# The two directions of a recurrent scan, summed by a transfer that adds in HBM

## The chip, the cores and the metric

The kernel runs on one core of a Trainium2 chip. That core has five engines with a queue each: TensorE (PE, matrix products into PSUM), VectorE (DVE), ScalarE (ACT), GpSimd (POOL) and SyncE (SP), which here only issues transfers. Each engine works through its own queue in order, and waits where another engine or a transfer has not signalled yet. The metric is the time of one launch in device microseconds; less is better. Before the change three runs took 1267.52, 1268.32 and 1270.27 us, a median of 1268.32 us.

## The reference, cut to what matters

The program is a two-layer backbone over 1024 latent tokens and 256 context tokens of width 1024. Layer 0 has a convolution branch A and a branch B, a gated linear recurrence that runs over the tokens in both directions. The change touches branch B alone, and the order of work in branch A's convolution.

```python
def lru_coeffs(u2, p):                     # u2: the input and its reversal
    r = sigmoid(u2 @ w_r + b_r); i = sigmoid(u2 @ w_i + b_i)      # 8 heads of 128
    log_a = -LRU_C * r * softplus(-lam)
    return exp(log_a), sqrt(-expm1(2 * log_a)) * (i * u2)

def rglru_branch(xb, p, h0, with_outputs):
    u = depthwise_conv(xb, p["sconv_w"], p["sconv_b"], (2, 1))    # 4 taps
    a, bx = lru_coeffs(stack([u, u[:, ::-1]]), p)
    hT, hs = lru_scan(a, bx, h0, with_outputs)                    # h = a * h + bx
    return hs[:, :, 0] + hs[::-1, :, 1], hT                       # the sum of the two directions

y_a = silu(layernorm(depthwise_conv(va * sigmoid(vg), conv_w, conv_b))) * silu(ga)   # 31 taps
y_b = rglru_branch(xb, p, h_ctx, True) * silu(gb)
out = concatenate([y_a, y_b]) @ w_out
```

The recurrence runs over the 256 context tokens first, and its last state starts the latent tokens. All products are made in float32 precision out of three matmuls of rounded parts (high by high, high by low, low by high).

## The kernel before

Channels lie on the 128 partitions and tokens along them, so the width of 1024 makes eight blocks j = 0 to 7. The stage at issue is a loop over these blocks (line 903), some 42.5 us a round. In round j TensorE makes, in this order: the gate input `vg` of branch A (two halves of 512 tokens), the value `va` (two halves), then, for block j + 1, the recurrence's input `xb` on the context (`xbc`), and then, interleaved, the gate products of block j (`g`, twelve groups of three matmuls, `gate_steps`) and `xb` of block j + 1 on the latent tokens. Each product of 512 columns is 24 matmuls: for each of eight blocks of the width `hi` by `xh`, `hi` by `xl`, `lo` by `xh`. Weights are loaded raw by SP, and `raw_split` makes their two parts: the high one `wh_...` by a cast on ACT, the low one `wl_...` by a subtraction on POOL. So TensorE's third matmul of a product is the first to need POOL's part.

The recurrence of block j is prepared in round j (gates into the buffers `l`) and finished in round j + 1 as `state`: POOL multiplies the input gate by the input (`rec_input`, one call for each direction: `l<-l,uc`), ACT makes `tanh` of the decay gate into a buffer `roots` (`rec_tanh`, `l<-l,chalf`), then `exp` and the square root, POOL multiplies again (`rec_scaled`, `l<-l,l`), and DVE scans (`rec_scan`: a multiply, then a scan over 256 and one over 1024 tokens, for each direction). At last `rec_sum` (line 877) adds the two directions on DVE and SP stores the sum to `yb_raw[j]` in HBM, from where `gated` (line 1219) reads it in the stage after the loop.

Six buffers `l` of 1280 columns are passed around. After its scans, a state's two results `i0` (forward) and `i1` (backward) become the `roots` of the next state:

```python
998                (r0, i0, r1, i1), (e, f) = state[2], state[3]
999                gates, roots = [e, f, r0, r1], [i1, i0]
```

So the `tanh` of direction 0, early in the round after, writes the buffer that held the backward result of the state before.

DVE also makes branch A's 31-tap convolution, block by block, as single steps of a generator; `fill(n)` puts the next n of them into DVE's queue at the place where it is called. The order on every engine in this stage is the order in which the program is written (each instruction is held behind the last of its engine, `on`). In a round the calls that matter come so: `vg` half 0; `rec_input(state, 1)`; the `first_tap` of the 4-tap convolution on ACT; `rec_tanh(state)`; the split of `va`'s weights; `vg` half 1; `va`; `xbc`; the scans and the sum; the gate products, and after the tenth of their twelve groups (`n == 9`, line 1006) the split of the next `vg` weights and `rec_input(now, 0)`; at the end `fill(6)`.

After the loop come the gate products `gb1` to `gb7` of branch B, with the last state's scans (block 7) among them, then the product `wob` with the gated branch B.

## Time and profile before

| | |
|---|---|
| median of the three runs | 1268.32 us |
| the three runs | 1267.52 to 1270.27 us |
| span of the profiled execution | 1263.6 us, 16209 instructions |
| PE busy | 1249.8 us (99%) |
| DVE busy | 1139.3 us (90%) |
| ACT busy | 653.8 us (52%) |
| POOL busy | 295.7 us (23%) |
| granted TensorE clock, mean | 0.998 |

The profile's times count from the span's start, and the span begins with the first instruction and ends with the last; the time of a run lies about 4.7 us above it (1268.32 against 1263.6). The profiled execution has no other time of its own. Matmuls are pipelined: one of 512 columns is shown with some 0.39 us, though the next one starts 0.23 us after it. In the rows an engine's idle time stands in brackets with what ended it. A transfer's time is counted from its issue to its landing. The loop over the blocks fills the span from about 75 to 414 us; the `gb` products end at about 490 us.

### The profile page before, as it was taken

The numbers are of one execution on the slowest core, as the hardware profiler recorded it, in microseconds if no ns is written. First come the engines' busy times: TensorE is split into PE (matmuls) and PEld (weight loads), VectorE is DVE, ScalarE is ACT, GpSimd is POOL, SyncE is SP. The second block draws the span as 40 slices with busy tenths as digits, with TensorE's granted clock in tenths as the row PEclk, the third lists the DMA queues.
The fourth block names the chain that finished last, engine by engine and source line by source line (L and its number), as shares of the span: only waits on it lengthen the run. The fifth ranks groups of instructions, "written<-read, shape, count | busy, mean of one in ns | idle before, by whom it ended". The sixth has DMA issues, their size and how long they took to land.

```text
span 1263.6 us, 16209 instructions
## 1 busy us (share of the span) xinstructions
PE 1249.8 (99%) x5866; PEld 1035.6 (82%) x5866; DVE 1139.3 (90%) x1746; ACT 653.8 (52%) x952; POOL 295.7 (23%) x176
## 2 busy tenths in 40 slices
PE   9999999999999999999999999999999999999997
PEld 7788888888888888888887878888888888888786
DVE  7799999999999999998978969999899987977975
ACT  8464566656666534237535445744343444644642
POOL 0015364436444547543210023000000000000002
PEclk9999999999999999999999999999999999999999
DMA  9970121112121233442436666344323334759723
GB/s 376 388 254 33 52 65 46 63 43 75 42 84 42 84 119 132 159 150 84 147 112 225 202 206 183 103 136 148 125 94 140 117 125 126 268 199 335 285 71 134
DMA packets 78705, 182.29 MB, mean 144 GB/s; under 512 B 7712, under 2 KB 23328, under 8 KB 78624
## 3 DMA queue, kind: packets, MB, share of 16 engines
q1 hardware_dynamic: 67328, 172.33, 39.8%
q10 hardware_dynamic: 11296, 8.92, 2.2%
q8 instruction: 46, 0.75, 0.2%
q14 instruction: 35, 0.29, 0.1%
HBM read 137.18 MB, written 44.04 MB: 143 GB/s over the span
## 4 chain that ended last, share of the span: by engine, by line
PE 70%; DVE 18%; DMA 7%; issue 2%; ACT 2%; POOL 1%; SPq 0%; POOLq 0%; ACTq 0%; DVEq 0%
PE wob L670 7%; DVE conv L670 5%; PE va L670 5%; PE xb L670 4%; PE vg L670 4%; DVE l L670 3%; PE fold L670 3%; PE g L670 3%; PE qb_v L1153 2%; PE ga L670 2%; PE qb_g L1156 2%; PE ga L161 2%; PE qb_v L1156 2%; PE qb_g L1155 2%; PE qb_g L1153 2%
## 5 line engine op out<-in xcount | busy, mean ns | idle before, releaser
L670 DVE SCALAR_TENSOR_TENSOR conv<-u,sm,conv 128x505 f32<-128x505 f32 (+6 forms) x224 | 153.6, 744 | 1.0
L2045 POOL TENSOR_TENSOR o<-x,rr 128x256 f32<-128x256 f32 (+1 forms) x10 | 9.2, 952 | 448.4 <-ACT rr L2045 448.4
L670 ACT ACTIVATE l<-g,sm 128x512 f32<-128x512 f32 (+1 forms) x96 | 58.7, 619 | 57.7 <-PE g L670 57.0
L670 POOL TENSOR_TENSOR l<-l,l 128x1280 f32<-128x1280 f32 x16 | 47.1, 2967 | 25.6 <-ACT l L670 15.1
L670 PE MATMUL gb<-h0h,wl_gb 128*128 128x512 f32 x128 | 49.9, 390 | 0.4 <-POOL wl_gb L670 0.4
L670 PE MATMUL va<-h0h,wl_va 128*128 128x512 f32 x128 | 49.9, 390 | 0.2 <-DVE wl_va L670 0.2
L98 ACT CAST wq_g<-wr_g 128x512 fp32r<-128x512 f32 x48 | 28.2, 621 | 41.9 <-DMA wr_g<-wg 15.6
L670 PE MATMUL gb<-h0l,wh_gb 128*128 128x512 f32 x128 | 49.8, 389 | 0.0
L670 PE MATMUL gb<-h0h,wh_gb 128*128 128x512 f32 x128 | 49.8, 389 | 0.0
L670 PE MATMUL va<-h0l,wh_va 128*128 128x512 f32 x128 | 49.8, 389 | 0.0
L670 PE MATMUL va<-h0h,wh_va 128*128 128x512 f32 x128 | 49.8, 389 | 0.0
L670 PE MATMUL wob<-ybl,wh_wob 128*128 128x512 f32 x128 | 49.8, 389 | 0.0
L670 PE MATMUL wob<-ybh,wl_wob 128*128 128x512 f32 x128 | 49.8, 389 | 0.0
L670 PE MATMUL wob<-ybh,wh_wob 128*128 128x512 f32 x128 | 49.8, 389 | 0.0
L670 DVE TENSOR_TENSOR_SCAN l<-l,l 128x256 f32<-128x256 f32 (+1 forms) x32 | 48.7, 1521 | 1.1
L670 DVE SCALAR_TENSOR_TENSOR conv<-cL,wsum,conv 128x506 f32<-128x506 f32 (+3 forms) x70 | 48.1, 745 | 0.2
L670 POOL TENSOR_TENSOR l<-l,uc 128x1280 f32<-128x1280 f32 x16 | 47.6, 2999 | 0.0
L98 ACT CAST wq_wo<-wr_wo 128x512 fp32r<-128x512 f32 x48 | 28.6, 620 | 35.5 <-DVE wr_wo L1134 12.4
L98 ACT CAST wq_v<-wr_v 128x512 fp32r<-128x512 f32 x48 | 28.1, 620 | 33.7 <-DMA wr_v<-wfold 16.6
L670 PE MATMUL xb<-h0l,wh_xb 128*128 128x512 f32 x112 | 43.8, 391 | 0.0
L670 PE MATMUL xb<-h0h,wh_xb 128*128 128x512 f32 x112 | 43.8, 391 | 0.0
L670 POOL TENSOR_TENSOR wl_xb<-wr_xb,wh_xb 128x1024 fp32r<-128x1024 f32 x7 | 16.8, 2407 | 114.5 <-ACT wh_xb L670 114.5
(680 smaller groups left out, 4362.5 us busy)
## 6 DMA issues: line engine op xcount, KB each, us to landing
modw<-modW SPq DMA_DIRECT2D x16, 512.0 KB, 10.2
mod<-modT SPq DMA_DIRECT2D x32, 256.0 KB, 3.4
wr_v<-wfold SPq DMA_DIRECT2D x16, 512.0 KB, 4.0
wr_g<-wg SPq DMA_DIRECT2D x16, 512.0 KB, 4.3
wr_wo<-wo SPq DMA_DIRECT2D x16, 512.0 KB, 4.1
mod<-modT SPq DMA_DIRECT2D x14, 512.0 KB, 4.5
y_b<-y SPq DMA_DIRECT2D x24, 256.0 KB, 3.5
y_t<-y SPq DMA_DIRECT2D x24, 256.0 KB, 3.1
```

Of the source, the lines that this page charges most:

```text
L98: return (nc.scalar.copy(hi, src), eng.tensor_tensor(out=lo, in0=src, in1=hi.bitcast(F32), op=sub))
L161: mm(ps, hi[:, kc], xh[k][:, cols], start=(k == 0), stop=False)
L670: last[eng] = f(*args, **kw)
L1153: nc.tensor.matmul(ps, hi, xh[k], start=(first and k == 0), stop=False, skip_group_check=not first)
L1155: nc.tensor.matmul(ps, hi, xl[k], start=False, stop=False, skip_group_check=not first)
L1156: mm = nc.tensor.matmul(ps, lo, xh[k], start=False, stop=(k == KH - 1), skip_group_check=not first)
L2045: tail[eng] = f(*args, **kw)
```

## The change

`rec_sum` goes, and with it DVE's addition of the two directions, eight instructions in all. In its place `rec_store(state, d)` stores one direction. For d = 0 SP writes the forward result to `yb_raw[j]`, right behind the forward scan. For d = 1 POOL issues a transfer of the backward result to the same place that adds to what lies there (`accum_op=add`). In the loop this stands behind the next state's `rec_input(now, 0)`, behind the tenth gate group; the last state's stands behind `at_rest` after its second scan. The `fill` at the end of rounds 1 to 6 rises from 6 to 8 steps, and the one after `gb3`'s product falls from 24 to 18, so that the convolution's steps are the same in number and stand earlier.

```diff
+    def plus(dst, src):
+        on("pool", nc.gpsimd.dma_start, dst, src, accum_op=add)
+
...
-        def rec_sum(st):
-            hs, hb = st[2][1], st[2][3]
-            vec(nc.vector.tensor_tensor, out=hs[:, C:], in0=hs[:, C:], in1=hb[:, C:], op=add)
-            nc.sync.dma_start(yb_raw[st[0]], hs[:, C:])
+        def rec_store(st, d):
+            latent = st[2][2 * d + 1][:, C:]
+            if d == 0:
+                nc.sync.dma_start(yb_raw[st[0]], latent)
+            else:
+                plus(yb_raw[st[0]], latent)
...
             if state is not None:
-                for d in range(2):
-                    rec_scan(state, d)
-                rec_sum(state)
+                rec_scan(state, 0)
+                rec_store(state, 0)
+                rec_scan(state, 1)
             at_rest()
...
                 if n == 9:
                     w = raw_split(raw, name)
                     rec_input(now, 0)
+                    if state is not None:
+                        rec_store(state, 1)
             all_of(steps)
-            fill(19 if state is None else 6)
+            fill(19 if state is None else 6 if final else 8)
...
         gb_product(3, gws[3])
-        fill(24)
+        fill(18)
         rec_scan(state, 0)
+        rec_store(state, 0)
...
         rec_scan(state, 1)
-        rec_sum(state)
         at_rest()
+        rec_store(state, 1)
```

How the queues change is read from the two built programs. First POOL at the end of round 1, before (`wl_vg`, `wl_va`, `wl_xb` are the low parts of weights; `l<-l,uc` are the two calls of `rec_input`):

```order
L670 TENSOR_TENSOR wl_vg_1608<-wr_vg_1471,wh_vg_1607 128x1024
L670 TENSOR_TENSOR l_914<-l_914,uc_1159 128x1280
L670 TENSOR_TENSOR l_911<-l_911,uc_1159 128x1280
L670 TENSOR_TENSOR wl_va_1680<-wr_va_1677,wh_va_1679 128x1024
L670 TENSOR_TENSOR wl_xb_1720<-wr_xb_1717,wh_xb_1719 128x1024
```

and now:

```order
L670 TENSOR_TENSOR wl_vg_1607<-wr_vg_1471,wh_vg_1606 128x1024
L670 TENSOR_TENSOR l_914<-l_914,uc_1159 128x1280
L670 DMA yb_raw_85<-l_912 128x1024
L670 TENSOR_TENSOR l_911<-l_911,uc_1159 128x1280
L670 TENSOR_TENSOR wl_va_1682<-wr_va_1679,wh_va_1681 128x1024
L670 TENSOR_TENSOR wl_xb_1722<-wr_xb_1719,wh_xb_1721 128x1024
```

The adding transfer out of `l_912`, block 0's backward result, stands between the two input products, and everything that POOL does for `va`'s weights is behind it.

Next ACT at the turn from round 1 to round 2, with what each instruction waits for, before (`uc<-xb` is `first_tap`, the two `chalf` rows are `rec_tanh`, `wh_va` is the high part of `va`'s weights):

```order
L670 ACTIVATE l_911<-g_1_1_768_1620,sm 128x512 [waits PE_49]
L670 ACTIVATE uc_1498<-xb_1517,sm 128x1024 [waits PE_49]
L670 ACTIVATE l_912<-l_913,chalf 128x1280 [waits DVE_49,Activation_49]
L670 ACTIVATE l_910<-l_909,chalf 128x1280 [waits DMAHW5_49,Activation_49]
L670 CAST wh_va_1679<-wr_va_1677 128x1024 [waits DMAHW4_49]
```

and now:

```order
L670 ACTIVATE l_911<-g_1_1_768_1620,sm 128x512 [waits PE_49]
L670 ACTIVATE uc_1498<-xb_1516,sm 128x1024 [waits PE_49]
L670 ACTIVATE l_912<-l_913,chalf 128x1280 [waits DMASW0_49,Activation_49]
L670 ACTIVATE l_910<-l_909,chalf 128x1280 [waits DMAHW5_49,Activation_49]
L670 CAST wh_va_1681<-wr_va_1679 128x1024 [waits DMAHW4_49]
```

Nothing has moved here, but one wait is another: the first `tanh`, which writes `l_912`, waited for DVE and now waits for `DMASW0`, the completion of POOL's adding transfer. `DMAHW5` is SP's store out of `l_910`.

Last DVE in round 2, from the scans of block 1 on, before (the scans are printed as SCALAR_TENSOR_TENSOR on `l` with 256 and 1024 columns; `conv` and `u` rows are convolution steps):

```order
L670 SCALAR_TENSOR_TENSOR l_911<-l_909,l_911 128x1280
L670 SCALAR_TENSOR_TENSOR l_911<-l_909,l_911 128x256
L670 SCALAR_TENSOR_TENSOR l_911<-l_909,l_911 128x1024
L670 TENSOR_TENSOR l_914<-l_914,l_911 128x1024
L670 SCALAR_TENSOR_TENSOR edge_junk,edges<-u_1735,sm 128x8
L670 TENSOR_TENSOR cL<-u_1735 128x512
L670 SCALAR_TENSOR_TENSOR conv_0_1632<-cL,wsum,u_1400 128x512
L670 SCALAR_TENSOR_TENSOR u_1400<-u_1400,sm,conv_1_1633 128x512
L670 SCALAR_TENSOR_TENSOR conv_1_1633<-cL,wsum,conv_1_1633 128x511
```

and now:

```order
L670 SCALAR_TENSOR_TENSOR l_911<-l_909,l_911 128x1280
L670 SCALAR_TENSOR_TENSOR l_911<-l_909,l_911 128x256
L670 SCALAR_TENSOR_TENSOR l_911<-l_909,l_911 128x1024
L670 SCALAR_TENSOR_TENSOR edge_junk,edges<-u_1737,sm 128x8
L670 TENSOR_TENSOR cL<-u_1737 128x512
L670 SCALAR_TENSOR_TENSOR conv_1_1633<-cL,wsum,conv_1_1633 128x511
```

The addition `l_914<-l_914,l_911` is gone, and the two convolution steps that stood behind `cL` here have moved up, ahead of the scans.

## The prediction

> **What bounds the kernel now.** I read the page's busy shares first, then the busy time by stage, then TensorE's waits.

> ```profile
> PE 1249.8 (99%) x5866; PEld 1035.6 (82%) x5866; DVE 1139.3 (90%) x1746; ACT 653.8 (52%) x952; POOL 295.7 (23%) x176
> ...
> core 0: us, PE busy (x) PEld busy (x) DVE busy (x) ACT busy (x) POOL busy (x), PEclk, DMA share, GB/s
> ...
> 289.10:331.60 42.50, 42.50 (x206) 35.86 (x205) 40.30 (x51) 26.45 (x30) 20.20 (x9) 1.00 0.16 56
> 331.60:374.10 42.50, 42.50 (x206) 35.85 (x205) 42.04 (x55) 26.46 (x30) 20.63 (x9) 1.00 0.20 69
> 374.10:415.00 40.90, 40.90 (x187) 34.02 (x187) 40.38 (x51) 27.84 (x31) 21.48 (x9) 1.00 0.19 60
> 415.00:490.60 75.60, 75.15 (x332) 61.89 (x331) 73.53 (x102) 32.32 (x43) 42.41 (x22) 1.00 0.32 103
> ...
> 600.00:760.00 160.00, 158.69 (x715) 130.56 (x714) 136.72 (x249) 74.92 (x119) 21.50 (x14) 1.00 0.55 179
> ...
> PE gb L670 <- POOL wl_gb L670: 0.4, 1, 0.4
> ```

> The first figure of a window is its length, the second PE's busy time. In the loop's rounds both are equal: TensorE never waits. DVE's 40.30 to 42.04 us a round lie beside it with 0.5 us or more to spare. After the loop PE idles 0.45 us (415 to 490.6, one wait for POOL's `wl_gb`) and 1.31 us (600 to 760). So relief for DVE finds about 1.8 us of TensorE waiting to remove, while any new wait that reaches TensorE is paid in full.

> **What DVE loses and gains.**

> ```profile
> L670 DVE TENSOR_TENSOR l<-l,l 128x1024 f32<-128x1024 f32 x8 | 9.8, 1225 | 0.3
> ...
> L670 DVE SCALAR_TENSOR_TENSOR conv<-u,sm,conv 128x505 f32<-128x505 f32 (+6 forms) x224 | 153.6, 744 | 1.0
> ```

> Eight additions at 1.225 us go, 9.8 us in all. In rounds 1 to 6 two steps more at 0.744 us replace each: 2 x 0.744 - 1.225 = +0.26 us a round, at most 42.04 + 0.26 = 42.3 us of 42.5: still hidden by TensorE. The six steps fewer behind `gb3` give back 4.5 us. I count the relief as 0.7 us of the 1.8 us: the 0.45 us at `wl_gb`, whose chain begins with DVE, and a little of the rest. The bounds are 0 and 1.8 us. Were TensorE's cover gone, the 0.26 us would be paid six times, 1.6 us.

> **The new wait, followed through one turn of the loop.** The backward result's buffer is free for the next round's first `tanh` only when the adding transfer has landed, and that transfer is issued behind the input product. Here are POOL, ACT and PE where round 7 begins:

> ```profile
> 371.56 2.40 POOL L670 TENSOR_TENSOR wl_vg<-wr_vg,wh_vg 128x1024 fp32r<-128x1024 f32 x1 [14.34 <-DVE conv L670]
> ...
> 376.83 3.00 POOL L670 TENSOR_TENSOR l<-l,uc 128x1280 f32<-128x1280 f32 x1
> 379.77 2.43 POOL L670 TENSOR_TENSOR wl_va<-wr_va,wh_va 128x1024 fp32r<-128x1024 f32 x1
> ...
> 375.22 2.61 ACT L670 ACTIVATE l<-l,chalf 128x1280 f32<-128x1280 f32 x2
> 377.74 1.03 ACT L670 CAST wh_va<-wr_va 128x1024 fp32r<-128x1024 f32 x1
> 379.56 0.60 ACT L670 ACTIVATE sg<-vg 128x512 f32<-128x512 f32 x1 [0.78 <-PE vg L670]
> ...
> 384.80 0.39 PE L670 MATMUL va<-h0h,wh_va 128*128 128x512 f32 x1
> 385.02 0.39 PE L670 MATMUL va<-h0l,wh_va 128*128 128x512 f32 x1
> 385.25 0.39 PE L670 MATMUL va<-h0h,wl_va 128*128 128x512 f32 x1
> ```

> The first input product ends at 376.83, where the second begins. Call L the time from there until the transfer has landed and ACT may go on: POOL's own share of the issue, the transfer and its signal. `tanh` began at 375.22; now it begins at 376.83 + L. From its begin to the end of `wh_va` are 377.74 + 1.03 - 375.22 = 3.55 us, then some 0.1 us and 2.43 us of POOL for `wl_va`: 6.08 us. TensorE wants `wl_va` at 385.25, so `tanh` may begin at 379.17 at the latest, and L may be 2.34 us. What is longer is idle time of TensorE:

> stall = L - 2.3 us in each round.

> Queued behind the waiting `tanh` on ACT are the second `tanh`, `wh_va`, the sigmoids `sg` that free `vg`'s PSUM, the cast `uh` that DVE's `ul` needs, and the next weights; behind the transfer on POOL the second input product and `wl_va`. The second input product now ends near 379.83 plus POOL's issue time, so ACT's cast, not POOL, sets `wl_va` as long as L exceeds the issue. The rest has slack: `exp` and the roots move by L + 1.6 us, but TensorE moves by L - 2.3 us too, and ACT had 3.9 us idle ahead of the next context tap.

> ```profile
> 356.33 0.57 ACT L670 ACTIVATE uc<-xbc,sm 128x256 f32<-128x256 f32 x1 [3.90 <-PE xbc L670]
> ...
> 365.29 3.08 DVE L670 TENSOR_TENSOR_SCAN l<-l,l 128x256 f32<-128x256 f32 x2
> ```

> DVE is held at `ul` for about as long as TensorE is, and both move on together. The transfer's other two waits are over by then: the backward scans of the state before end at 368.4, 8 us ahead of 376.83, and the forward store is issued earlier still.

> Seven `tanh` stand behind a transfer: those of rounds 2 to 7 and the last state's among the `gb` products. For the last one the same chain leads to `gb2`'s low weights, with one consequence more:

> ```profile
> 412.94 2.61 ACT L670 ACTIVATE l<-l,chalf 128x1280 f32<-128x1280 f32 x2
> ...
> 413.52 5.91 POOL L670 TENSOR_TENSOR l<-l,uc 128x1280 f32<-128x1280 f32 x2
> ...
> 423.23 5.91 POOL L670 TENSOR_TENSOR l<-l,l 128x1280 f32<-128x1280 f32 x2 [1.45 <-ACT l L670]
> 429.08 2.42 POOL L670 TENSOR_TENSOR wl_gb<-wr_gb,wh_gb 128x1024 fp32r<-128x1024 f32 x1
> ...
> 435.73 0.39 PE L670 MATMUL gb<-h0h,wl_gb 128*128 128x512 f32 x1
> ```

> The first of the two input products ends at 413.52 + 2.96 = 416.48. `tanh` goes from 412.94 to 416.48 + L, so the roots, POOL's scaled products and the `wl_gb` behind them (end 431.50) move by 3.54 + L, to 435.04 + L. TensorE wants them at 435.73 plus its own stall of L - 2.35, 433.38 + L. That is 1.6 us more, once, whatever L is. The last state's own transfer is waited for only by a load of `cH` and by reads of `yb_raw`, which the earlier forward store leaves room for: nothing.

> **How long is L?** The trace has no transfer that adds and none that POOL issues. The nearest rows, with median time to landing at the end:

> ```profile
> yb_raw<-l SPq DMA_DIRECT2D x8, 512.0 KB, 2.6
> wr_vg<-win SPq DMA_DIRECT2D x7, 512.0 KB, 3.5
> modw<-modW SPq DMA_DIRECT2D x16, 512.0 KB, 10.2
> ```

> Below, the plain store of the same tile, 2.6 us: adding cannot be less work. Reading HBM first and writing then would be a load and a store in a row, 3.5 + 2.6 = 6.1 us. Above, the slowest transfers of this size, 10.2 us beside full traffic; here traffic is light (a DMA share of 0.2). I take L = 5.3 us, nearer the sum than the store, since reads and writes of the pieces overlap in part while POOL's issue comes on top. The stall is then 3.0 us.

> [...]

> **The sum.** 7 x 3.0 = 21.0, plus 1.6, minus 0.7: +21.9 us. The profiled span would be 1263.6 + 21.9 = 1285.5 us; the median lies 4.7 us above the span, so 1290 us. With L = 2.6: 7 x 0.3 + 0.9 = 3.0, 1271 us. With L = 10.2: 7 x 7.9 + 0.9 = 56.2, 1324 us.

> **Rivals.** *The transfer is nearly as quick as the store* (L below 3.3). For it: an idle DMA, and the store's 2.6 us. Against it: it reads as well, and POOL must issue it. Stall below 1.0, 1271 to 1279 us.

> *POOL issues the transfer while the product in front still runs.* Then L counts from 373.9, not from 376.83: with L = 5.3 the transfer lands at 379.2, `tanh` may begin until 379.17, and nothing stalls. The 1.6 us at `gb3` go as well, since the roots come 2.96 us earlier. What is left is DVE's relief, 0.7 to 1.8 us: 1266.5 to 1267.6 us. This is the mechanism on the other side, and it decides from an overlap of 2.9 us on. For it: POOL's rows follow each other with no gap, so something of the next instruction is prepared early. Against it: two products in a row take 5.9 us, twice one, so their work does not overlap.

> *TensorE's clock falls in the stalls.* The profile's end shows what idling does:

> ```profile
> 1254.00:1255.00 1.00, 0.61 (x4) 0.52 (x4) 0.59 (x2) 0.30 (x2) 0.31 (x1) 1.00 0.97 322
> ...
> 1257.00:1258.00 1.00, 0.00 (x0) 0.00 (x0) 0.80 (x3) 0.16 (x1) 0.76 (x2) 0.68 0.41 139
> 1258.00:1260.00 2.00, 0.00 (x0) 0.00 (x0) 1.24 (x4) 0.00 (x0) 1.33 (x2) 0.50 0.48 157
> ```

> The granted clock, third from the end, goes from 1.00 to 0.50 some 3 us after dense work stops near 1254.6. If each stall did that, and the clock took as long to return, 3 us at half speed cost 1.5 us more per stall, 10.5 us: 1301 us. Against it: the stall is split, about 0.9 us before the first matmul (`wh_va` at 385.7 instead of 384.80) and the rest before the third. [...]

> **How the numbers follow.** The forecast, with L from 3.3 to 7.0 and a full clock, 1276 to 1303 us, gets 0.66; a longer transfer or a falling clock, 1301 to 1324 us, 0.16; the quick transfer 0.10; the overlapped issue 0.08. Leaving out the overlapped issue, the lower half of the quick case and the far end of the long one, the range is 1274 to 1313 us. About 0.2% or 2.5 us is what a measurement of this kernel can tell from no change, so 1265.8 to 1270.9 us is "same". The overlapped issue falls there or just below it, 0.05 and 0.03, and the quick case ends above. Slower: 0.92.

> **What would show it.** In the changed profile the first `tanh` of rounds 2 to 7 should be released by the transfer of `yb_raw`, some 7 us later in its round than before, and PE should wait for ACT's `wh_va` and POOL's `wl_va`, seven times (`gb` once) about 3 us in all; each round should take 45.5 us instead of 42.5. DVE's 1.225 us additions should be gone with no gain to be seen. If `tanh` begins in time, or PE shows no wait for `va` weights, the central step is wrong; if the transfer's time to landing is far from 5 us, only the size is.

## The result, and the profile after

The changed kernel takes 1300.88 us (median of 4 runs, 1296.27 to 1305.84), the kernel before, on the same chip, 1267.92 us: a ratio of 1.0263, 95% interval 1.0235 to 1.0291. That is 33.0 us more; the forecast was 21.7 us more. The profiled execution took 1300.49 us, with a span of 1298.7 us, 35.1 us above the span of before.

The page of the changed kernel, busy shares and three of its groups (the number behind the last bar is the idle time of the engine just before the group, and what ended it):

```profile
PE 1263.3 (97%) x5866; PEld 1039.9 (80%) x5866; DVE 1136.3 (87%) x1738; ACT 652.8 (50%) x952; POOL 303.8 (23%) x184
...
L670 PE MATMUL va<-h0h,wl_va 128*128 128x512 f32 x128 | 52.7, 412 | 10.4 <-POOL wl_va L670 10.2
...
L670 PE MATMUL va<-h0h,wh_va 128*128 128x512 f32 x128 | 52.4, 410 | 3.6 <-ACT wh_va L670 3.6
...
L670 ACT ACTIVATE l<-l,chalf 128x1280 f32<-128x1280 f32 x16 | 21.0, 1358 | 48.1 <-DMA yb_raw<-l 48.1
```

TensorE, never idle in the loop before, now waits for both parts of `va`'s weights, and ScalarE's `tanh` waits 48.1 us for the transfer of `yb_raw`. DVE's additions are gone and its share is lower, with no gain to be seen. TensorE's waits in total, times and longest:

```profile
PE va L670 <- POOL wl_va L670: 10.2, 6, 1.7
PE gb L670 <- POOL wl_gb L670: 4.5, 3, 1.8
PE va L670 <- ACT wh_va L670: 3.6, 6, 0.8
PE qac_wo L1164 <- DVE wq_wo L99: 2.3, 2, 1.3
```

Round 7 in the order of time, for POOL, ACT and PE, answers to the rows that the prediction shows of before:

```profile
393.98 2.94 POOL L670 TENSOR_TENSOR l<-l,uc 128x1280 f32<-128x1280 f32 x1
396.87 0.84 POOL L670 DMA_DIRECT2D yb_raw<-l  x1
397.48 3.23 POOL L670 TENSOR_TENSOR l<-l,uc 128x1280 f32<-128x1280 f32 x1
405.47 2.36 POOL L670 TENSOR_TENSOR wl_va<-wr_va,wh_va 128x1024 fp32r<-128x1024 f32 x1 [4.76 <-ACT wh_va L670]
...
401.84 2.62 ACT L670 ACTIVATE l<-l,chalf 128x1280 f32<-128x1280 f32 x2 [6.46 <-DMA yb_raw<-l]
404.37 1.03 ACT L670 CAST wh_va<-wr_va 128x1024 fp32r<-128x1024 f32 x1
...
405.45 0.50 PE L670 MATMUL va<-h0h,wh_va 128*128 128x512 f32 x1 [0.44 <-ACT wh_va L670]
405.79 0.40 PE L670 MATMUL va<-h0l,wh_va 128*128 128x512 f32 x1
407.89 0.50 PE L670 MATMUL va<-h0h,wl_va 128*128 128x512 f32 x1 [1.71 <-POOL wl_va L670]
```

The transfer is issued at 396.87, when the first input product has ended, and the `tanh` starts at 401.84: L = 4.97 us here, 5.0 to 5.3 us over the seven turns. `wh_va` and `wl_va` follow in a chain, and TensorE waits 0.44 us for the one and 1.71 us for the other. The round loses more than their sum, 2.7 us: the idle time in brackets counts from the end at which the matmul before is shown, 0.39 us after its start, where the next one would start after 0.23; and behind each wait the second matmul starts 0.34 us after the first (405.45 and 405.79).

But not all turns are alike. Where TensorE's same matmul stands in both traces gives what each stretch lost:

| stretch | lost against before, us |
|---|---|
| up to round 1 | 0.6 |
| rounds 2, 4, 6 | 4.70, 4.53, 4.56 |
| rounds 3, 5, 7 | 2.87, 2.78, 2.72 |
| `gb` products | 7.4 |
| `wob` to the end | 4.9 |
| sum | 35.1 |

The waits are of the same size in every round. What is more in every other one is seen in the windows around the waits of round 2 (first three rows) and of round 3 (last three). A row is a stretch with its length, TensorE's busy time, the matmuls in it and the granted clock; the stretches are 3.41 us long and begin where the clock's records begin and end:

```profile
core 0: us, PE busy (x), PEclk, DMA share, GB/s
170.50:173.91 3.41, 2.67 (x12) 1.00 0.00 0
173.91:177.33 3.42, 1.64 (x6) 1.00 0.00 0
177.33:180.74 3.41, 3.41 (x10) 0.50 0.33 84
...
218.28:221.70 3.42, 2.81 (x12) 1.00 0.00 0
221.70:225.11 3.41, 1.73 (x8) 1.00 0.21 51
225.11:228.52 3.41, 3.41 (x17) 1.00 0.20 51
```

Behind round 2's waits the clock is 0.50 for exactly one stretch (10 matmuls where there are 17 at full clock); behind round 3's it stays at 1.00. It fell so four times, behind the waits of rounds 2, 4 and 6 and of `gb2`. A round with the fall lost 4.60 us on average and one without 2.79, so a fall cost 1.8 us: 3.41 us at half speed are 1.71.

In the `gb` stage there is one more wait, at `gb5`, where the prediction had counted nothing (POOL, then SP's queue, ACT and PE):

```profile
472.86 0.88 POOL L670 DMA_DIRECT2D yb_raw<-l  x1 [8.86 <-DVE l L670]
479.32 3.01 POOL L670 TENSOR_TENSOR ybl<-sb,ybh 128x512 fp32r<-128x512 f32 x2 [5.58 <-DMA yb_raw<-l]
485.88 2.37 POOL L670 TENSOR_TENSOR wl_gb<-wr_gb,wh_gb 128x1024 fp32r<-128x1024 f32 x1 [3.56 <-issue]
...
479.38 0.33 SPq L256 DMA_DIRECT2D cH<-cc  x1
...
483.70 0.63 ACT L257 ACTIVATE cH<-cH 128x512 f32<-128x512 f32 x1 [2.46 <-DMA cH<-cc]
...
484.71 1.04 ACT L670 CAST wh_gb<-wr_gb 128x1024 fp32r<-128x1024 f32 x1
...
485.81 0.50 PE L670 MATMUL gb<-h0h,wh_gb 128*128 128x512 f32 x1 [0.16 <-ACT wh_gb L670]
488.31 0.50 PE L670 MATMUL gb<-h0h,wl_gb 128*128 128x512 f32 x1 [1.77 <-POOL wl_gb L670]
```

POOL's first `ybl` (the low part of block 0's gated branch) waits 5.58 us for the last adding transfer, and SP issues the load of `cH` only when that has landed, too. The second is what reaches TensorE. The load lands some 4 us later, ACT's step on `cH` waits 2.46 us for it, `wh_gb` of `gb5` stands behind that step on ACT, and `wl_gb` behind `wh_gb`; POOL itself stood idle for 3.56 us between `ybl` and `wl_gb`. TensorE waits 0.16 + 1.77 = 1.93 us.

### The profile page after: what moved, and what is told of

It is laid out like the page before. It is cut to its first block, busy times and chain, and to the rows that moved or that the text cites. A ratio compares the mean times of both kernels' runs of the same rounds, so it can differ in the third digit from the quotient of the medians.

```text
span 1298.7 us, 16234 instructions
## 1 busy us (share of the span) xinstructions
PE 1263.3 (97%) x5866; PEld 1039.9 (80%) x5866; DVE 1136.3 (87%) x1738; ACT 652.8 (50%) x952; POOL 303.8 (23%) x184
## 5 line engine op out<-in xcount | busy, mean ns | idle before, releaser
L670 DVE SCALAR_TENSOR_TENSOR conv<-u,sm,conv 128x505 f32<-128x505 f32 (+6 forms) x224 | 152.7, 745 | 0.8
L670 ACT ACTIVATE l<-g,sm 128x512 f32<-128x512 f32 (+1 forms) x96 | 58.5, 618 | 58.0 <-PE g L670 54.5
L670 PE MATMUL va<-h0h,wl_va 128*128 128x512 f32 x128 | 52.7, 412 | 10.4 <-POOL wl_va L670 10.2
L670 POOL TENSOR_TENSOR l<-l,l 128x1280 f32<-128x1280 f32 x16 | 47.6, 2998 | 38.7 <-ACT l L670 38.7
L670 PE MATMUL va<-h0h,wh_va 128*128 128x512 f32 x128 | 52.4, 410 | 3.6 <-ACT wh_va L670 3.6
L670 PE MATMUL gb<-h0h,wl_gb 128*128 128x512 f32 x128 | 50.9, 398 | 4.5 <-POOL wl_gb L670 4.5
L670 PE MATMUL va<-h0l,wh_va 128*128 128x512 f32 x128 | 51.8, 405 | 0.0
L670 DVE TENSOR_TENSOR_SCAN l<-l,l 128x256 f32<-128x256 f32 (+1 forms) x32 | 50.7, 1586 | 1.1
L670 PE MATMUL gb<-h0h,wh_gb 128*128 128x512 f32 x128 | 50.8, 397 | 0.7 <-ACT wh_gb L670 0.7
L670 PE MATMUL gb<-h0l,wh_gb 128*128 128x512 f32 x128 | 50.4, 394 | 0.0
L670 PE MATMUL wob<-ybh,wh_wob 128*128 128x512 f32 x128 | 49.9, 389 | 0.0
L670 PE MATMUL wob<-ybl,wh_wob 128*128 128x512 f32 x128 | 49.9, 389 | 0.0
L670 PE MATMUL wob<-ybh,wl_wob 128*128 128x512 f32 x128 | 49.8, 389 | 0.0
L670 POOL TENSOR_TENSOR l<-l,uc 128x1280 f32<-128x1280 f32 x16 | 49.3, 3085 | 0.0
L670 DVE SCALAR_TENSOR_TENSOR conv<-cL,wsum,conv 128x506 f32<-128x506 f32 (+3 forms) x70 | 47.4, 743 | 0.1
L670 ACT ACTIVATE l<-l,chalf 128x1280 f32<-128x1280 f32 x16 | 21.0, 1358 | 48.1 <-DMA yb_raw<-l 48.1
L670 PE MATMUL xb<-h0l,wh_xb 128*128 128x512 f32 x112 | 43.9, 392 | 0.0
L670 PE MATMUL xb<-h0h,wh_xb 128*128 128x512 f32 x112 | 43.8, 391 | 0.0
L670 PE MATMUL xb<-h0h,wl_xb 128*128 128x512 f32 x112 | 43.6, 389 | 0.0
## 6 DMA issues: line engine op xcount, KB each, us to landing
modw<-modW SPq DMA_DIRECT2D x16, 512.0 KB, 10.2
wr_v<-wfold SPq DMA_DIRECT2D x16, 512.0 KB, 3.8
wr_g<-wg SPq DMA_DIRECT2D x16, 512.0 KB, 4.6
wr_wo<-wo SPq DMA_DIRECT2D x16, 512.0 KB, 4.8
mod<-modT SPq DMA_DIRECT2D x14, 512.0 KB, 4.6
```

Of the source, the lines that this page charges most:

```text
L670: last[eng] = f(*args, **kw)
```

## The experiments

The theory after the result: (1) the next `tanh` waits for the landing of the adding transfer, and only through that do the weights come late; (2) where enough of the wait falls into one of the clock's stretches, TensorE runs the next one at half speed; (3) the last transfer costs the wait at `gb5`. The rivals: the moved convolution steps cost; POOL's issue or the transfer's traffic costs wherever it stands; the clock falls by chance. Every ratio is against runs of the kernel before in the same comparison, medians of 1266.5 to 1267.4 us.

**fills_only**: the convolution steps as changed, the sum back on VectorE.

```diff
                 rec_scan(state, 0)
-                rec_store(state, 0)
                 rec_scan(state, 1)
+                rec_sum(state)
...
                     rec_input(now, 0)
-                    if state is not None:
-                        rec_store(state, 1)
```

and the same for the last state, with `rec_sum` as it was.

> The sum of the two directions goes back to VectorE and SP as before the change; only the other part of the change stays: 8 instead of 6 convolution steps at the end of rounds 1 to 6, and 18 instead of 24 behind the third gb product. Theory (the landing of the adding transfer holds the next tanh, and nothing else costs): 2 x 0.744 = 1.5 us more for VectorE in a round, under TensorE's 42.5 us; the time is that of before, 1266 to 1270 us, with TensorE waiting in no round of the loop. Rival (the moved convolution steps hold VectorE's chain, and through it TensorE): a good part of the 33 us shows here, 1275 us or more.

Measured: 1267.50 us, ratio 0.9994 (0.9983 to 1.0005), and no wait of TensorE in the loop. The steps moved cost nothing and bring nothing.

**transfer_only**: the transfers as changed, the convolution steps as before.

```diff
-            fill(19 if state is None else 6 if final else 8)
+            fill(19 if state is None else 6)
...
-        fill(18)
+        fill(24)
```

> The two transfers stay as changed; the convolution steps go back to 6 in every round and 24 behind the third gb product. Theory (landing): the seven stalls stay as they are, 1298 to 1303 us, within 3 us of the changed kernel. Rival (the moved convolution steps cost): near 1270 us.

Measured: 1302.29 us, ratio 1.0274 (1.0254 to 1.0295). The whole loss is the transfers'. Here L is 5.2 to 5.4 us, and the clock fell behind the waits of rounds 2 (for two stretches), 4, 5, 7 and `gb2`: other rounds than in the changed kernel.

**early**: the same transfer, issued ahead of the split of the `vg` weights.

```diff
                 if n == 9:
+                    if state is not None:
+                        rec_store(state, 1)
                     w = raw_split(raw, name)
                     rec_input(now, 0)
-                    if state is not None:
-                        rec_store(state, 1)
```

> In the loop the adding transfer is issued ahead of the split of the next vg weights and of the first input product instead of behind them; the same transfers, bytes and convolution steps, and the last state's transfer stays where it is. POOL stands idle there, so the transfer starts when the backward scan has ended, some 8 us earlier. Theory (landing): with 5.1 us from issue to landing it is over 3 us before the tanh could start; no round stalls, the clock stays at 1.00 in the loop, and what is left is the end of the gb stage (some 2 us) and at most a few us behind it: 1267 to 1274 us. Rival (the adding transfer disturbs wherever it runs, by its traffic or by POOL's issue): most of the 33 us stays, 1290 us or more.

Measured: 1269.91 us, ratio 1.0021 (1.0009 to 1.0033): 30 of the 33 us are gone. ACT at the turn to round 7 and POOL in the `gb` stage, in the order of time:

```profile
375.30 2.61 ACT L670 ACTIVATE l<-l,chalf 128x1280 f32<-128x1280 f32 x2
377.81 1.05 ACT L670 CAST wh_va<-wr_va 128x1024 fp32r<-128x1024 f32 x1
...
444.43 0.88 POOL L670 DMA_DIRECT2D yb_raw<-l  x1 [10.99 <-DVE l L670]
450.85 3.04 POOL L670 TENSOR_TENSOR ybl<-sb,ybh 128x512 fp32r<-128x512 f32 x2 [5.54 <-DMA yb_raw<-l]
456.68 2.38 POOL L670 TENSOR_TENSOR wl_gb<-wr_gb,wh_gb 128x1024 fp32r<-128x1024 f32 x1 [2.79 <-issue]
```

`tanh` begins without a wait, 0.1 us from its time of before (375.22), and the clock is at 1.00 through the loop. It is a near thing: the transfer lands only 0.7 to 2.2 us ahead of the `tanh` in rounds 2 to 7, where over 3 us had been expected, and the last state's `tanh`, among the `gb` products, waits 1.3 us for it, which doesn't reach TensorE. The transfers are the same in number and bytes; so neither traffic nor POOL's issue is what costs. Of TensorE's waits this one, at `gb5`, stays from the `gb` stage (here too it is ACT's step on `cH` that waits for its load, 1.73 us):

```profile
PE gb L670 <- POOL wl_gb L670: 1.4, 1, 1.4
```

**plain**: the transfer in its place, but it only writes.

```diff
-                plus(yb_raw[st[0]], latent)
+                on("pool", nc.gpsimd.dma_start, yb_raw[st[0]], latent)
```

> The backward direction's transfer on POOL, in the same place, only writes and does not add; so the sum of the two directions is left out. Theory A (the adding is what makes it long, a read of HBM and then a write): from the end of the input product to the tanh 3.0 to 4.0 us instead of 5.1, stalls of 0.7 to 1.7 us, no fall of the clock, 1273 to 1283 us. Theory B (it is the way of a transfer that POOL issues, whatever it does at the end): 4.7 to 5.2 us, stalls of 2.4 to 2.9 us with the clock falling in some, 1294 to 1303 us.

Measured: 1277.49 us, ratio 1.0075 (1.0057 to 1.0093). POOL, then ACT, at the turn to round 7:

```profile
382.52 0.59 POOL L670 DMA_DIRECT2D yb_raw<-l  x1
...
385.54 2.62 ACT L670 ACTIVATE l<-l,chalf 128x1280 f32<-128x1280 f32 x2 [4.51 <-DMA yb_raw<-l]
```

L is 3.0 to 3.2 us in six of seven turns, 2 us less than with the adding, and a round loses 0.8 to 1.0 us (one, where the transfer took 4.0 us, 1.8). Theory A holds in that the adding makes the transfer long; that a read of HBM is what the adding takes its time for, no run shows. Stall = L - 2.3, as the prediction has it, would be 0.7 to 0.9. In the loop the clock stayed whole, as expected; it fell once behind it, at `gb3`, where TensorE waited 2.52 us: 4.4 of the 10 us are lost there.

**swap**: the two buffers change places, so that the second `tanh` writes what the transfer reads.

```diff
-                gates, roots = [e, f, r0, r1], [i1, i0]
+                gates, roots = [e, f, r0, r1], [i0, i1]
```

> The buffers change places: the first tanh of a round writes the forward result's buffer, which SP's store has long left, and the second tanh the backward result's, which the adding transfer reads. Nothing else changes. Theory (landing): only the second tanh waits, and behind its start come 1.3 us of its own, 1.05 for wh_va, 0.1 and 2.43 for wl_va, 4.8 us instead of 6.1; so the stall is 5.1 - 3.65 = 1.5 us in each of seven turns, 10 us. By the windows of the traces so far (1.5 us of idle TensorE in one 3.41 us window left the clock alone, 1.9 us halved it) the clock stays at 1.00 in the loop, which takes another 6 to 7 us away. With 1 us at gb3, 2 at gb5 and 2 to 4 behind: 1267.4 + 10.3 + 5 to 7 = 1283 us, 1279 to 1287. Rival (POOL's queue, not the tanh, is what holds TensorE): unchanged, 1298 to 1304 us. Rival (only the first tanh matters): 1268 to 1274 us.

Measured: 1287.81 us, ratio 1.0169 (1.0154 to 1.0185), 0.8 us above the range. No fall of the clock in the loop, as expected; a round loses 1.7 to 2.1 us, not 1.5, since L was 5.2 to 5.5 us here. Round 4 lost 2.8, where the input product ahead of the transfer took 3.5 us instead of 3.0, and round 3 lost 1.5 us more behind a late `ul` of VectorE, whose copy `cL` had taken 3.5 us instead of 0.7. The window of the longest wait of round 3, and the next:

```profile
216.73:220.15 3.42, 1.72 (x9) 1.00 0.00 0
220.15:223.56 3.41, 3.41 (x16) 1.00 0.24 77
```

In the `gb` stage, the rest of the miss, `gb3` waited for POOL and the clock fell once behind it (DVE, POOL, then PE):

```profile
448.26 4.22 DVE L670 SCALAR_TENSOR_TENSOR l<-l,l 128x1280 f32<-128x1280 f32 x1 [4.58 <-POOL l L670]
...
451.10 3.59 POOL L670 TENSOR_TENSOR wl_gb<-wr_gb,wh_gb 128x1024 fp32r<-128x1024 f32 x1
...
454.74 0.50 PE L670 MATMUL gb<-h0h,wl_gb 128*128 128x512 f32 x1 [2.53 <-POOL wl_gb L670]
```

`wl_gb` took 3.59 us instead of the 2.42 of before. VectorE's multiply ahead of the scan ran beside it, and was itself 4.22 us long instead of 1.48; before, the multiply came after `wl_gb` had ended. So the wait at `gb3` is 2.5 us where the clock was whole; it was 0.97 us in the changed kernel, where the fall at `gb2` had made TensorE later.

**swap_behind**: as swap, and the second `tanh` stands behind `wh_va` and `sg` on ACT.

```diff
-                rec_tanh(state)
+                rec_tanh(state, (0,))
...
             act(sg[0], vg[0], AF.Sigmoid)
+            if state is not None:
+                rec_tanh(state, (1,))
...
-        rec_tanh(state)
+        rec_tanh(state, (0,))
         gb_weights(2)
+        rec_tanh(state, (1,))
```

> As the kernel with the buffers in changed places, and the second tanh stands on ScalarE behind the cast of wh_va and the sigmoid sg of vg's first half instead of ahead of them. The transfer is issued where the change has it. Theory (landing): the transfer ends near 381.9 on the times of before, ScalarE has 2.5 us of idle time ahead of the cast uh, and the exponentials come only at 388; so no weights of va wait and no round stalls. What is left is gb3, gb5 and behind: 1268 to 1273 us. Rival (the transfer itself, its place on POOL or its traffic): 1290 us or more.

Measured: 1275.18 us, ratio 1.0066 (1.0050 to 1.0083), 2 us above the range. In the loop nothing is lost at all, though the transfer stands where the change put it and takes 5.2 to 5.6 us: it is the waiting `tanh` ahead of the weights, and nothing else, that costs there. The `gb` stage loses 6.4 us: 3.50 us of waiting at `gb3`, with a fall of the clock behind it, and 1.51 at `gb5`. I had not worked through `gb3`, where the roots now come later. The rest lies behind the `gb` stage, where the profiled execution lost 5.8 us, with one more fall of the clock at 1163 us, far from the change.

**late**: the transfer stands behind the second input product as well.

```diff
                 rec_input(state, 1)
+                if before is not None:
+                    rec_store(before, 1)
                 fill(2)
```

`before` is the state before, handed on from round to round; the transfer at its old place goes, and the last of the seven is moved likewise among the `gb` products.

> The adding transfer is issued one product later, behind the second input product (3.0 us), with the tanh still waiting for it. Theory (landing): the stall grows by the product, from 2.8 to 5.8 us in each of seven turns, 21 us more; and since TensorE then idles 3.7 us in a row ahead of wh_va, each stall fills most of a 3.41 us window wherever the windows lie, so the clock is halved in every turn, once or twice (1.7 us each), not in four of seven: 5 to 18 us more. 1301 + 21 + 5 to 18 = 1327 to 1340 us. Rival (the stalls come from POOL's issue or from traffic): 1296 to 1306 us, as changed. Rival (the clock falls by chance, in about half the turns as before): near 1322 us.

Measured: 1330.74 us (2 runs), ratio 1.0504 (1.0485 to 1.0524), in the range. The waits of round 3 in windows:

```profile
224.32:227.73 3.41, 0.37 (x2) 1.00 0.00 0
227.73:231.14 3.41, 1.88 (x5) 0.50 0.08 10
231.14:234.56 3.42, 3.42 (x9) 0.50 0.34 89
```

The clock fell in all seven turns, for two stretches each. The rivals are out: the stall follows the place of the transfer, and with stalls of this length the clock fell every time.

**early_tail**: early in the loop (its edit is as above), and the last state summed on VectorE as before the change.

```diff
         rec_scan(state, 0)
-        rec_store(state, 0)
...
         rec_scan(state, 1)
-        at_rest()
-        rec_store(state, 1)
+        rec_sum(state)
+        at_rest()
```

> The transfer early in the loop, as in the kernel that issues it ahead of the vg weights, and the last state (block 7) summed on VectorE and stored by SP as before the change. Theory (the last transfer's landing holds POOL's first ybl, and behind it wl_gb5, 1.4 us of TensorE there): that wait for wl_gb goes and the gb stage ends 1 to 2 us earlier than with the transfer early alone (1269.9 us): 1266.5 to 1269 us. Rival (what that kernel lost against before lies behind the gb stage): the wait goes, and the time stays at 1269 to 1271 us. If VectorE's relief were worth anything, this kernel would show it: below 1266 us.

Measured: 1266.87 us, ratio 1.0003 (0.9992 to 1.0014). The wait at `gb5` is gone, and the time is that of before: the last transfer cost 2 to 3 us by the medians, of which the trace shows the wait of 1.4. (The two kernels were measured in different comparisons, and the intervals of their ratios just overlap.) VectorE's relief, seven of its eight additions with the moved steps and here without a cost to TensorE, is worth nothing that can be measured. It is the best version with the transfer, and no better than the kernel before.

**half** and **half_plain**: half the columns, added (first edit) and only written (second).

```diff
-                plus(yb_raw[st[0]], latent)
+                plus(yb_raw[st[0]][:, :H], latent[:, :H])
...
-                plus(yb_raw[st[0]], latent)
+                on("pool", nc.gpsimd.dma_start, yb_raw[st[0]][:, :H], latent[:, :H])
```

> The adding transfer carries only the first 512 of the 1024 columns (256 KB); the other half of the backward result is left out of the sum. In the same place as changed. Theory S (what adding costs, some 2.2 us beside the plain transfer's 3.05, grows with the bytes): 3.5 to 4.0 us from the input product's end to the tanh, stalls of 1.2 to 1.7 us, no fall of the clock in the loop, 1278 to 1285 us. Theory F (adding costs a fixed trip, a read ahead of the write): 4.6 to 5.1 us, stalls of 2.3 to 2.8 us and some falls of the clock, 1292 to 1301 us.

> The same 256 KB, written and not added: the sum is left out in that half as well, and the forward result is overwritten there. It gives the base for the half-size adding transfer. Theory S: 2.3 to 2.6 us from the input product's end to the tanh, stalls near 0.2 us. Theory F: 2.7 to 3.0 us, stalls of 0.4 to 0.7 us. Either way 1268 to 1278 us.

Measured: half 1284.06 us (2 runs, ratio 1.0137, 1.0097 to 1.0177), half_plain 1279.51 us (one run). The transfers, size and median time from issue to landing, of the changed kernel (SP's plain store and POOL's adding one), then of plain, of half and of half_plain:

```profile
yb_raw<-l SPq DMA_DIRECT2D x8, 512.0 KB, 2.6
yb_raw<-l POOLq DMA_DIRECT2D x8, 512.0 KB, 5.0
```

```profile
yb_raw<-l POOLq DMA_DIRECT2D x8, 512.0 KB, 3.0
```

```profile
yb_raw<-l POOLq DMA_DIRECT2D x8, 256.0 KB, 3.9
```

```profile
yb_raw<-l POOLq DMA_DIRECT2D x8, 256.0 KB, 2.4
```

Half the bytes save 0.6 us of a plain transfer and 1.1 of an adding one; the adding itself costs 2.0 us at 512 KB and 1.5 at 256. So it is neither only by the bytes nor fixed: a line through the two gives 1.0 us fixed and 1.0 us for 512 KB. The split is rough: with 5.3 us, the median of the adding transfer in most of the other traces, it is 0.7 and 1.6. From the input product's end to the `tanh` the seven turns took 3.7 to 4.2 us in half and 2.4 to 2.6, once 2.9, in half_plain: Theory S, at the upper end of its ranges and a little over. half's stalls were 1.6 to 1.9 us, above the 1.2 to 1.7 expected, and against the expectation the clock fell once in the loop, in round 3, which lost 4.0 us. half_plain's time is above its range for another reason: in one round a convolution step, usually 0.74 us, took 3.51 (DVE, then POOL),

```profile
316.59 3.51 DVE L670 SCALAR_TENSOR_TENSOR conv<-cL,wsum,u 128x512 f32<-128x512 f32 x1
...
313.67 5.88 POOL L670 TENSOR_TENSOR l<-l,l 128x1280 f32<-128x1280 f32 x2 [3.01 <-ACT l L670]
```

TensorE waited 3.0 us, the clock fell, and the round lost 4.9 us by it. The step began together with POOL's second product and ended 0.55 us behind it; the last section has more such cases.

## Why the prediction was right, and where it was not

The direction, the mechanism in the loop and the place were right; the sum was 11 us short, by a fall of the clock that the forecast had left out and a wait that it had put at nothing.

- **TensorE bounds the kernel, and relief for DVE is worth little.** Right. 0.7 us was forecast; fills_only and early_tail show none beyond 0.1%.
- **The first `tanh` of seven turns waits for the landing.** Right: early, swap and swap_behind each take away another link of the chain (the late issue, the buffer of the first `tanh`, the weights behind the second), and the stalls go as the chain says.
- **L = 5.3 us, the stall 3.0 us.** Right: 5.0 to 5.3 us and 2.8 us in the turns with the clock whole; seven are 19.6 us, not 21.0. The estimate between a store (2.6) and a load and store in a row (6.1) was sound: adding costs 2.0 us over the plain 3.0. That it hit so closely is partly luck, since nothing fixed the place between the two bounds: that the reads and writes of the pieces overlap in part was my assumption, and no run shows it.
- **The clock stays whole, since the stall is split: this step failed.** I put TensorE's clock falling into the rivals, and argued that 0.9 us ahead of the first matmul and the rest ahead of the third are no long gap. The gap need not be in one piece: in transfer_only two of 1.12 and 1.06 us in one stretch brought a fall (the last section has the count). The clock fell in four of seven turns, some 7 us. The rival's price of 1.5 us was near the 1.8 measured, but not its count, all seven; that its 1301 us is the measured time is luck, and comes of terms that neither case had.
- **The 1.6 us at `gb3`.** Its size was off: 0.97 us, because the fall at `gb2` held TensorE back; with the clock whole 2.5 us, since `wl_gb` took 3.6 us there, beside VectorE's multiply, instead of the 2.42 of before.
- **The last state's own transfer, put at nothing: this step failed.** I named the load of `cH` that waits for it, but did not follow what stands behind that load: ScalarE's step on `cH`, `wh_gb` and `wl_gb` of `gb5`. It is 1.93 us in the changed kernel; early_tail gives it back.
- **"The median lies 4.7 us above the span": off.** The changed kernel's runs lie 1.7 to 1.9 us above their spans; before's profiled execution, by the same step, was some 2.5 us shorter than the median. That is most of why the spans differ by 35.1 and the medians by 33.0. The forecast's step of 21.9 us is not touched by it.

Summed: 19.6 for the stalls, 7 for the clock, 1.0 at `gb3`, 1.9 at `gb5`, less 0.45 for the wait that went, 29 us. Some 4 us of the 33 remain. The span of the changed kernel lost 4.9 us behind the `gb` stage, with waits for `wq_wo` and `fo` that before's profile doesn't have. That is no clear effect of the change: against the same profiled execution of before, the ten experiments lost 0.1 (swap) to 5.8 us (swap_behind) there, and fills_only and early_tail, which are as quick as before by their medians, 2.2 and 4.2. What the rest is stays open.

## What to carry to other kernels

The adding transfer held the buffer that it reads until it had landed, and the `tanh` that writes that buffer next, a loop's turn later, waited on its queue with everything behind it (seven times; 48.1 us of ScalarE's idle time ended with it): follow the buffer, not only the data, and issue the transfer as soon as its source is there (30 of 33 us came back when two lines were moved). An adding transfer of 512 KB took 5.0 to 5.4 us (medians of seven traces) where a plain one took 3.0 from the same queue and 2.6 from SP, so it pays only if the engine that it relieves sets the time, which DVE did not. A stall on a dense TensorE may cost more than its length (a round of the changed kernel lost 4.60 us with a fall of the clock and 2.79 without), so price the clock with it.

## What the runs showed of the hardware that I had not expected

POOL's issue of an adding transfer takes 0.84 to 1.04 us in the records, of a plain one 0.6 (0.76 the first). The next product on POOL starts 0.6 us after the issue has begun (0.8 at the first), and takes 3.2 us behind an adding transfer instead of 3.0: the queue itself is held for about 1 us at most.

Some instructions of VectorE and POOL were stretched where they ran beside each other, as at `gb3` of swap (3.59 us instead of 2.42 on POOL, 4.22 instead of 1.48 on VectorE). Between 75 and 491 us of the twelve traces, 69 instructions of VectorE lasted over 1 us longer than the median of their form, half_plain's step and swap's `cL` among them. Every one of them overlapped a two-input product or subtraction of POOL, and ended 0.02 to 1.35 us, mostly 0.55, behind the end of one; 3267 others overlapped one and were not stretched so. That VectorE then waits for POOL's instruction to end is my guess, and no run was made to try it.
